# Unread products added to TensorE behind the last layer of a hybrid trunk

## The chip, the core and the metric

The kernel runs on one core of one Trainium2 chip. The metric is the device time of one execution in microseconds (us); the time before is 1177.72 us, the median of two runs (1177.52 and 1177.92). Five engines work side by side, each through its own instruction stream: TensorE (PE; its weight loads are listed apart as PEld), VectorE (DVE), ScalarE (ACT), GpSimd (POOL) and SyncE (SP, which issues DMAs here).

## What is computed

Two layers of a decoder trunk over 256 tokens of width 1024, in float32:

```python
proj = x @ w_in[l]                                  # 1024 -> 12800
y_a = short_conv_mixer(parts[3], parts[4], parts[5], conv_w[l])
y_b = dilated_attention_mixer(parts[6:6 + n_attn], positions)   # 3 groups of 8 heads of 64
y_c = chunked_spatial_gating(parts[6 + n_attn], parts[7 + n_attn], ...)
m = g_a * (y_a @ p_a[l]) + g_b * (y_b @ p_b[l]) + g_c * (y_c @ p_c[l])
x = layer_norm(ALPHA * x + m @ w_o[l], ln1_g[l], ln1_b[l])
h = jax.nn.silu(x @ w_gate[l]) * (x @ w_up[l])      # 1024 -> 2816
x = layer_norm(ALPHA * x + h @ w_down[l], ln2_g[l], ln2_b[l])
```

## The kernel before

Each float32 matrix product is made of three products of 12-bit parts in the type float32r: with h + l the two parts of an operand, h h' + h l' + l h'. Weights come from HBM in panels of up to 1 MB into one of three `raw` buffers (SP issues them, line 158) and are split there in pieces of 512 columns: ScalarE writes the high part `wh` (line 179), VectorE the low part `wl` (line 180). The pieces live in `slots`, 72 of 2 KB a partition, which the activations share.

Two patterns carry nearly all products. `feat` (lines 246 to 248, through `mm3`) has features on partitions: the weights are stationary (128x128), the activations move, 256 columns, one for each token; a panel of 256 features takes 2 x 8 x 3 = 48 products. `toks` (lines 266 to 268) has tokens on partitions: 128 tokens of an activation are stationary, the weights move, 512 columns (256 in the first two feed-forward blocks). Names in the profile stand as out<-moving,stationary or the reverse; `xh` and `xl` are the parts of x, `yah`, `ych`, `hh`, `mh` and their like those of branch results, hidden features and the merged branches, all kept in slots.

Where operands lie follows from the pools: `xh` and `xl` begin 160 bytes past a multiple of 512 in each partition, every slot and every `raw` buffer 224 bytes past one, and rows inside are multiples of 512 bytes apart. With "distance" for the moving operand's address less the stationary one's, modulo 512 bytes, `feat` on x has distance 448, `toks` on x has 64, and both have 0 where the activation lives in slots.

Between runs of products other work is placed by a clock of the program's own: transposes (lines 296, 612, 804; two to four in a row into a `trp` bank), attention's products (scores of 64 rows, lines 591 to 595; values of 64 weight columns, line 622). PSUM holds four `acc` banks and four `trp` banks, taken in turn.

The end: `down_last` finishes the last product into the four `acc` banks, a token tile after the other. For each half row VectorE adds it to x (`resid`, line 337) and takes statistics; `norm` (lines 313 to 327) follows for the tile, and SP stores each half (line 855). After that the program ends with a barrier of all engines.

Of the kernel before, what the change touches and what calls it, by code (L numbers as in the profile page):

```python
# [18 lines left out]
S = 256  # L19
# [20 lines left out]
# Weights: columns split at a time, panels loaded ahead.  # L40
PIECE = 512
RAW = 3
# Slots of 2 KB a partition; those that weights leave to others.
NS = 72
SPARE = 8
# TensorE time between two turns of the other engines' work, ns.
TICK = 1300
# Pieces of weights to have ready for splits to wait behind a layer norm.
# [5 lines left out]
# Steps of attention a turn.  # L54
PACE = 0.5

# Column layout of the constants.
# [8 lines left out]
# Pieces, of few bits each, of 2*pi and of (2**20, 2**9)/(2*pi) less its whole turns.  # L66
# [6 lines left out]
def constants():  # L73
    """Identity, masks and rotary frequencies: they depend on shapes alone."""
# [3 lines left out]
    # Attention keeps tokens ordered by their residue mod 2, in two tiles: a tile of queries sees  # L78
    # all keys of the first group, and of the dilated ones only the keys of its own tile.
# [16 lines left out]
def trunk(ctx: ExitStack, tc: tile.TileContext, a, out):  # L96
# [43 lines left out]
    # ---------------------------------------------------------------- weights  # L140
# [3 lines left out]
    class Panel:  # L144
        """Weights [kc * 128, nw], kept as 12-bit parts h + l in pieces of 512 columns."""
# [23 lines left out]
        def at(self, k, c, n):  # L169
            """Columns c..c+n of row block k, both parts."""  # L170
# [6 lines left out]
    def split(h, l, src):  # L177
        """h + l = src, both of them of 12 bits."""
        nc.scalar.activation(h, src, AF.Copy)  # L179
        V.tensor_tensor(l, src, h.bitcast(F32), op=OP.subtract)  # L180
# [15 lines left out]
    def used(n=1):  # L196
        """Pieces of weights done with."""
        free(2 * n)
# [6 lines left out]
    def soon(n, f):  # L205
        """f at the n-th turn from here."""
        timed.append((clock[1] + n, f))

    def tick():
        """Work of other engines, and attention, between runs of matmuls."""  # L210
# [33 lines left out]
    def mm3(o, hl, rhs_h, rhs_l, first, last):  # L244
        """o (+)= h.T @ (h' + l') + l.T @ h'."""
# [4 lines left out]
    def feat(p, rhs):  # L250
        """Features on partitions: (panel).T @ activations, a bank for two blocks."""
# [11 lines left out]
    def toks(ps, lhs, p, k, c, n, first, last):  # L263
        """Tokens on partitions: activations.T @ panel, one row block into one bank."""
# [10 lines left out]
    def by_residue(x):  # L275
        """Tokens (innermost) in the order of attention."""
# [15 lines left out]
    def to_features(t, q):  # L292
        """Half of x of a token tile, transposed and split."""
# [6 lines left out]
    # ---------------------------------------------------------------- layer norm  # L300
# [642 lines left out]
```

## Time and profile before

| | before |
|---|---|
| time, median of 2 runs | 1177.72 us |
| span of the profiled execution | 1174.9 us |
| PE busy | 1164.0 us, 99% of the span, 8884 products |
| PEld busy | 1101.0 us, 94% |
| DVE busy | 789.3 us, 67% |
| ACT busy | 622.8 us, 53% |
| POOL busy | 14.2 us, 1% |
| granted TensorE clock, mean | 0.999 of full speed |
| DMA | 222.41 MB, mean 189 GB/s |

The span runs from the first to the last instruction of one execution. A product's duration in the profile includes its way through the array, so durations overlap; what a run of products costs is read from starts, as the pitch from one start to the next. In a timeline row the columns are: start in us from the span's start, duration in us, engine, line, operation, out<-in, partitions x columns, count of instructions that the row merges, and in brackets the idle time before.

### The profile page before, as it was taken

How to read it: one execution, taken by the hardware profiler on the slowest of the kernel's cores; microseconds unless marked ns; L12 is line 12 of the kernel's file. 1: busy time of each engine (PE TensorE's matmuls, PEld its weight loads, DVE VectorE, ACT ScalarE, POOL GpSimd, SP SyncE). 2: the span in 40 equal slices, each digit the busy share in tenths (PEclk: the TensorE clock that was granted, in tenths of full speed). 3: DMA queues.
4: the chain of work that ended last, by engine and by line, in shares of the span. 5: the costliest groups of instructions: out<-in, count | busy, mean ns of one | idle time of the engine just before them, and what ended most of it. 6: DMA issues, size and time to landing. Idle time of an engine off the chain costs nothing.

```text
span 1174.9 us, 21651 instructions
## 1 busy us (share of the span) xinstructions
PE 1164.0 (99%) x8884; PEld 1101.0 (94%) x8884; DVE 789.3 (67%) x1426; ACT 622.8 (53%) x1126; POOL 14.2 (1%) x29
## 2 busy tenths in 40 slices
PE   9999999999999999999999999999999999999997
PEld 7899999999999899998888999999999999999985
DVE  6978886666755777556496677766676567764534
ACT  6666554676544466445185454546755444654530
POOL 0000000000000000000100000000000000000000
PEclk9999999999999999999999999999999999999999
DMA  9588554435857378448367664453566583774530
GB/s 343 202 258 251 171 167 146 142 126 197 265 178 235 111 228 281 171 146 317 113 215 250 181 188 135 151 172 109 177 216 204 194 251 108 253 234 160 176 111 36
DMA packets 180695, 222.41 MB, mean 189 GB/s; under 512 B 5456, under 2 KB 154228, under 8 KB 180596
## 3 DMA queue, kind: packets, MB, share of 16 engines
q1 hardware_dynamic: 178500, 214.66, 55.7%
q0 software_dynamic: 1952, 6.31, 1.9%
q8 instruction: 69, 1.13, 0.4%
q14 instruction: 30, 0.25, 0.1%
q10 hardware_dynamic: 144, 0.07, 0.0%
HBM read 213.67 MB, written 1.05 MB: 183 GB/s over the span
## 4 chain that ended last, share of the span: by engine, by line
PE 98%; DVE 1%; DMA 0%; ACT 0%; SPq 0%; issue 0%
PE acc L246 22%; PE acc L247 21%; PE acc L248 21%; PE acc L267 9%; PE acc L268 9%; PE acc L266 9%; PE acc L622 1%; PE trp L595 1%; PE trp L612 1%; PE trp L592 1%; PE acc L701 1%; PE trp L296 0%; DMA raw<-in_w_in 0%; PE trp L591 0%; PE trp L804 0%; PE trp L442 0%
## 5 line engine op out<-in xcount | busy, mean ns | idle before, releaser
L180 DVE TENSOR_TENSOR wl<-raw,wh 128x512 fp32r<-128x512 f32 x776 | 490.9, 686 | 179.8 <-ACT wh L179 171.2
L246 PE MATMUL acc<-xh,wh 128*128 128x256 f32 x1856 | 523.1, 282 | 0.0
L247 PE MATMUL acc<-xl,wh 128*128 128x256 f32 x1856 | 514.9, 277 | 0.0
L248 PE MATMUL acc<-xh,wl 128*128 128x256 f32 x1856 | 514.8, 277 | 0.0
L179 ACT ACTIVATE wh<-raw 128x512 fp32r<-128x512 f32 x776 | 432.1, 622 | 69.7 <-DMA raw<-in_w_in 26.5
L246 PEld LDWEIGHTS acc<-xh,wh 128*128 128x128 f32 x1856 | 348.8, 188 | 6.0 <-issue 2.1
L248 PEld LDWEIGHTS acc<-xh,wl 128*128 128x128 f32 x1856 | 349.8, 188 | 0.0
L247 PEld LDWEIGHTS acc<-xl,wh 128*128 128x128 f32 x1856 | 348.8, 188 | 0.1
L266 PE MATMUL acc<-wh,xh 128*128 128x512 f32 (+1 forms) x288 | 100.4, 349 | 0.3 <-ACT xh L179 0.3
L267 PE MATMUL acc<-wl,xh 128*128 128x512 f32 (+1 forms) x288 | 98.8, 343 | 0.2 <-DVE wl L180 0.2
L268 PE MATMUL acc<-wh,xl 128*128 128x512 f32 (+1 forms) x288 | 98.8, 343 | 0.0
L266 PE MATMUL acc<-wh,hh 128*128 128x512 f32 x176 | 68.6, 390 | 0.0
L268 PE MATMUL acc<-wh,hl 128*128 128x512 f32 x176 | 68.5, 389 | 0.0
L267 PE MATMUL acc<-wl,hh 128*128 128x512 f32 x176 | 68.5, 389 | 0.0
L266 PEld LDWEIGHTS acc<-wh,xh 128*128 128x128 f32 x288 | 54.7, 190 | 7.2 <-ACT wh L179 0.5
L267 PEld LDWEIGHTS acc<-wl,xh 128*128 128x128 f32 x288 | 54.8, 190 | 6.8 <-DVE wl L180 0.5
L268 PEld LDWEIGHTS acc<-wh,xl 128*128 128x128 f32 x288 | 54.7, 190 | 6.6 <-DVE xl L180 0.4
L599 ACT ACTIVATE p<-p,ml 128x512 f32<-128x512 f32 x32 | 23.3, 728 | 61.3 <-DVE ml L598 56.3
L179 ACT ACTIVATE hh<-hs 128x512 fp32r<-128x512 f32 x18 | 11.4, 634 | 64.3 <-DVE hs L823 64.3
L316 ACT ACTIVATE sd<-mv,eps 128x1 f32<-128x1 f32 x12 | 3.6, 298 | 72.4 <-DVE mv L313 72.4
L337 DVE SCALAR_TENSOR_TENSOR xt<-xt,acc 128x512 f32<-128x512 f32 x16 | 11.0, 685 | 44.5 <-PE acc L268 44.5
L268 PEld LDWEIGHTS acc<-wh,hl 128*128 128x128 f32 x176 | 33.0, 188 | 6.8
(148 smaller groups left out, 1329.1 us busy)
## 6 DMA issues: line engine op xcount, KB each, us to landing
raw<-in_w_in SPq DMA_DIRECT2D x99, 1024.0 KB, 5.3
raw<-in_w_gate SPq DMA_DIRECT2D x22, 1024.0 KB, 5.8
raw<-in_w_up SPq DMA_DIRECT2D x22, 1024.0 KB, 5.2
raw<-in_w_down SPq DMA_DIRECT2D x22, 1024.0 KB, 4.8
raw<-in_p_a SPq DMA_DIRECT2D x8, 1024.0 KB, 5.3
raw<-in_p_c SPq DMA_DIRECT2D x8, 1024.0 KB, 5.1
raw<-in_w_o SPq DMA_DIRECT2D x8, 1024.0 KB, 5.7
sw<-qk SPq DMA_DIRECT2D x96, 64.0 KB, 3.0
```

What stands on the lines that cost most here:

```text
L179: nc.scalar.activation(h, src, AF.Copy)
L180: V.tensor_tensor(l, src, h.bitcast(F32), op=OP.subtract)
L246: nc.tensor.matmul(o, lhsT=hl[0], rhs=rhs_h, start=first, stop=False)
L247: nc.tensor.matmul(o, lhsT=hl[0], rhs=rhs_l, start=False, stop=False)
L248: nc.tensor.matmul(o, lhsT=hl[1], rhs=rhs_h, start=False, stop=last)
L266: nc.tensor.matmul(ps, lhsT=lhs[0], rhs=h, start=first, stop=False)
L267: nc.tensor.matmul(ps, lhsT=lhs[0], rhs=l, start=False, stop=False)
L268: nc.tensor.matmul(ps, lhsT=lhs[1], rhs=h, start=False, stop=last)
L592: nc.tensor.matmul(ps[:, c], lhsT=q[d, b, own], rhs=qk[hf, "kh"][d, b, keys], start=False, stop=True)
L595: nc.tensor.matmul(ps[:, c], lhsT=q[d, b, own], rhs=k[d, b, keys], start=True, stop=True)
L599: nc.scalar.activation(p, p, AF.Exp, bias=ml[:, 0:1], scale=-1.0, accum_out=ml[:, 1:2])
L612: nc.tensor.transpose(ps[:, i * 128:(i + 1) * 128], p[:, i * 128:(i + 1) * 128], ident)
```

## The change

Behind the last layer's program, two `raw` buffers `W` are filled with ones by POOL, and products follow on TensorE whose results nothing reads. A first loop runs over 18 distances `d` from 0 to 480 bytes: `mm3` as in `feat`, on the parts of x as moving operand and a piece of `W` as stationary one, whose offset `o` is set so that the distance is `d`; 24 products, two transposes (`kick(2)`), and the 24 again. A second loop does the pattern of `toks` at the same distances, 12 products each, with x stationary and `W` moving. Then come products of 64 rows, of 64 columns and of both, as attention has them, on x's parts and on the constants (float32), and four transposes. The other hunks take comments and docstrings out; line numbers stay as they were up to line 920.

```diff
@@ -920,6 +920,60 @@
     assert not hooks and not slow and live[0] == 0, (len(hooks), live)
 
 
+
+    W = []
+    for i in range(2):
+        w = wp.tile([128, 2048], F32R, tag="raw", name="w")
+        nc.gpsimd.memset(w.bitcast(F32), 1.0)
+        W.append(w)
+
+    def kick(n):
+        ps = trp()
+        for i in range(n):
+            nc.tensor.transpose(ps[:, i * 128:(i + 1) * 128], con[:, C_M:C_M + 128], ident)
+
+    dist = (0, 16, 32, 48, 64, 96, 128, 160, 192, 224, 256, 288, 320, 352, 384, 416, 448, 480)
+    ps = acc()
+    for d in dist:
+        o = (-64 - d) % 512 // 4
+        for again in range(2):
+            for k in range(8):
+                wk = [w[:, k * 256 + o:k * 256 + o + 128] for w in W]
+                mm3(ps[:, :S], wk, *xf(k), k == 0, k == 7)
+            if again == 0:
+                kick(2)
+    for d in dist:
+        o = (-64 + d) % 512 // 4
+        for k in range(4):
+            h, l = (w[:, k * 256 + o:k * 256 + o + 512] for w in W)
+            lhs = xtok(k, 0)
+            nc.tensor.matmul(ps, lhsT=lhs[0], rhs=h, start=k == 0, stop=False)
+            nc.tensor.matmul(ps, lhsT=lhs[0], rhs=l, start=False, stop=False)
+            nc.tensor.matmul(ps, lhsT=lhs[1], rhs=h, start=False, stop=k == 3)
+    b4 = [trp() for i in range(4)]
+    up, dn = slice(0, 64), slice(64, 128)
+    m = con[:, C_M:]
+    for i in range(6):
+        nc.tensor.matmul(b4[0][:, :256], lhsT=xh[up, 0, :128], rhs=xh[up, 1, :], start=True, stop=True)
+    for i in range(3):
+        for j, r in enumerate((up, dn)):
+            nc.tensor.matmul(b4[j][:, :256], lhsT=xh[r, 0, :128], rhs=xh[r, 1, :], start=True, stop=True)
+    for i in range(4):
+        for j, r in enumerate((up, dn)):
+            nc.tensor.matmul(b4[j + 2][:, i % 4 * 128:(i % 4 + 1) * 128], lhsT=m[r, :128], rhs=m[r, 256:384], start=True, stop=True)
+    for i in range(4):
+        for j, r in enumerate((up, dn)):
+            for q in (up, dn):
+                nc.tensor.matmul(b4[j][q, i * 64:(i + 1) * 64], lhsT=m[r, q], rhs=m[r, 256:320], start=True, stop=True)
+    for i in range(4):
+        for q in (up, dn):
+            nc.tensor.matmul(b4[2][q, i * 128:(i + 1) * 128], lhsT=m[:, q], rhs=m[:, 256:384], start=True, stop=True)
+    for i in range(4):
+        for q in (up, dn):
+            nc.tensor.matmul(b4[3][q, i * 64:(i + 1) * 64], lhsT=m[:, q], rhs=m[:, 256:320], start=True, stop=True)
+    kick(4)
+
+
```

In the order of TensorE's instructions the new ones stand behind the last product of `down_last` (a row is line, operation, out<-moving operand, partitions x columns; the weights aren't named; line 246 to 248 is `mm3`, `w` one of the two buffers `W`):

```order
 L267 MATMUL acc<-wl,hh_13579 128x512
 L268 MATMUL acc<-wh,hl_13580 128x512
-L939 UNCONDITIONAL_BRANCH
+L246 MATMUL acc<-xh,w 128x256
+L247 MATMUL acc<-xl,w 128x256
+L248 MATMUL acc<-xh,w 128x256
```

The program went to its closing branch there; now the first of 1172 products follow. Their end, on the same engine:

```order
+L952 MATMUL acc<-w,xl 128x512
+L957 MATMUL trp<-xh 128x256 x6
+L960 MATMUL trp<-xh 128x256 x6
+L963 MATMUL trp<-con 128x128 x8
+L967 MATMUL trp<-con 64x64 x16
+L970 MATMUL trp<-con 64x128 x8
+L973 MATMUL trp<-con 64x64 x8
+L933 MATMUL trp<-con 128x128 x4
+L993 UNCONDITIONAL_BRANCH
```

The last forms stand behind the second loop, and only then does TensorE reach its closing branch. On POOL, whose last work was the load of the last norm's parameters:

```order
 L306 DMA gb<-in_ln_g 128x512 x2
 L306 DMA gb<-in_ln_b 128x512 x2
-L939 UNCONDITIONAL_BRANCH
-L939 ISA
+L927 MEMSET w 128x2048 x2
+L993 UNCONDITIONAL_BRANCH
+L993 ISA
```

The two fills come behind those loads. The first product waits for VectorE (the residual that reads the first `acc` bank) and for POOL's first fill, the third product for the second fill. The streams of ScalarE, VectorE and SP are as before.

## Rows read from the trace of the kernel before

**Rows 1.** The page: granted clock in 40 slices (tenths), and chain by engine.
```profile
PEclk9999999999999999999999999999999999999999
PE 98%; DVE 1%; DMA 0%; ACT 0%; SPq 0%; issue 0%
```
**Rows 2.** Timeline, the end: last product, first residual behind it, last norm step, store.
```profile
1165.77 0.39 PE L268 MATMUL acc<-wh,hl 128*128 128x512 f32 x1
...
1166.19 0.69 DVE L337 SCALAR_TENSOR_TENSOR xt<-xt,acc 128x512 f32<-128x512 f32 x1 [4.02 <-PE acc L268]
...
1170.89 0.75 DVE L327 SCALAR_TENSOR_TENSOR xt<-xt,sd,gb 128x512 f32<-128x512 f32 x1
1171.67 0.33 SPq L855 DMA_DIRECT2D out<-xt  x1
```
**Rows 3.** DMA issues: count, KB each, median us to landing.
```profile
out<-xt SPq DMA_DIRECT2D x4, 256.0 KB, 2.0
```
**Rows 4.** Timeline: last splits, POOL's last load, residual that frees the first bank.
```profile
1126.52 2.73 DVE L180 TENSOR_TENSOR wl<-raw,wh 128x512 fp32r<-128x512 f32 x4 [2.11 <-ACT wh L179]
...
1132.32 0.54 POOL L306 DMA_DIRECT2D gb<-in_ln_b  x1 [0.23 <-issue]
...
1149.88 0.69 DVE L337 SCALAR_TENSOR_TENSOR xt<-xt,acc 128x512 f32<-128x512 f32 x1 [20.63 <-PE acc L268]
```
**Rows 5.** Groups by line and form, VectorE's fills: busy us, mean ns of one.
```profile
L898 DVE MEMSET idle<- 128x64 f32 x1 | 0.1, 112 | 0.8 <-PEq L931 0.8
L899 DVE MEMSET eps<- 128x1 f32 x1 | 0.1, 59 | 0.0
```
**Rows 6.** Timeline, layer 1's gates and branches: where runs on x and slots begin.
```profile
865.22 0.29 PE L246 MATMUL acc<-xh,wh 128*128 128x256 f32 x1
...
881.56 0.28 PE L246 MATMUL acc<-yah,wh 128*128 128x256 f32 x1
...
895.94 0.29 PE L246 MATMUL acc<-xh,wh 128*128 128x256 f32 x1
...
895.94 0.19 PEld L247 LDWEIGHTS acc<-xl,wh 128*128 128x128 f32 x1
```
**Rows 7.** Timeline, layer 1's feed-forward: first product behind a transpose's successor, and the end.
```profile
1008.40 0.28 PE L247 MATMUL acc<-xl,wh 128*128 128x256 f32 x1
...
1106.15 0.39 PE L266 MATMUL acc<-wh,hh 128*128 128x512 f32 x1
```
**Rows 8.** Timeline, two transposes amid products of 256 columns.
```profile
420.94 0.38 PE L804 MATMUL trp<-con,hs 128*128 128x128 f32 x2
421.07 0.36 PE L266 MATMUL acc<-wh,xh 128*128 128x256 f32 x1
421.28 0.28 PE L267 MATMUL acc<-wl,xh 128*128 128x256 f32 x1
```
**Rows 9.** Timeline, token products of 512 columns: starts of runs on x and hidden features.
```profile
585.79 0.39 PE L266 MATMUL acc<-wh,xh 128*128 128x512 f32 x1
...
594.72 0.49 PE L296 MATMUL trp<-con,xt 128*128 128x128 f32 x3
...
1160.56 0.39 PE L266 MATMUL acc<-wh,hh 128*128 128x512 f32 x1
```
**Rows 10.** Timeline, attention's products of 64 rows, and of 64 weight columns.
```profile
119.68 0.28 PE L591 MATMUL trp<-stack 128*128 128x256 f32 x1
119.89 0.38 PE L592 MATMUL trp<-kh,stack 64*128 64x256 f32 x1
120.11 0.60 PE L595 MATMUL trp<-qk,qk 64*128 64x128 f32 x4
120.65 0.38 PE L246 MATMUL acc<-xh,wh 128*128 128x256 f32 x1
...
164.02 1.09 PE L622 MATMUL acc<-pT,va 128*64 128x128 f32 x16
165.04 0.39 PE L246 MATMUL acc<-xh,wh 128*128 128x256 f32 x1
```

## Prediction

> **What bounds the kernel now.** I read the page first, then the end of the timeline, then stretches of TensorE's timeline. The page's chain of work that ended last is TensorE for 98% of the span, and its clock row stands at full speed (2.4 GHz) in every slice of 40 [rows 1]. So the time is the sum of TensorE's pitches (start of one product to the start of the next), and a product added at the end is paid in full unless it fits under something that already follows TensorE's last product. Such a thing exists and is short: the last product starts at 1165.77 us; VectorE's residual and layer norm follow until 1171.64, and the store is issued at 1171.67 for 0.33 us [rows 2] and lands some 2.0 us later [rows 3], at 1174.0; the span closes at 1174.87, another 0.9 us. From 1166.00 (1165.77 plus one pitch of 0.23) to 1174.87 are 8.9 us of cover; what TensorE does beyond that lengthens the run. The profiled execution's span is 1174.87 us; the median of the two runs is 1177.72, so 2.85 us lie around the span, which I keep.
>
> **What the change adds.** Nothing is moved or removed; by the order, the engines' programs are the same up to the end. Added are two fills on POOL and 1172 products on TensorE, with no reader. They start without a wait, if three things are in time. The accumulator bank that the first run takes is free once the residual of the first half row has read it, by 1150.57 us [rows 4]. The two raw buffers are free after the last splits, which end at 1129.25 [rows 4]. The fills stand on POOL behind its last load, which ends there at 1132.86 [rows 4]. No fill of this size is in the trace; the nearest rows are VectorE's fills of 64 columns (112 ns) and of one (59 ns) [rows 5], 0.84 ns a column, so 1.7 us for 2048 columns. Taken four times as slow, two fills still end near 1147, 19 us ahead of 1166.0. They cost nothing as long as each takes under 16.5 us; TensorE waits for whatever the two take beyond 33 us.
>
> **The price of a product of the layers' pattern.** The same instruction, 128x128 weights against 256 columns, runs at three steady pitches in the trace. With x as the moving operand (its address lies 448 bytes ahead of the weights', modulo 512): 144 products from 865.22 to 881.56, 113.5 ns each. With the split branch results as the moving operand (distance 0, since they and the weights live in the same slots): 120 products from 881.56 to 895.94, 119.8 ns each [rows 6]. And with x again, same distance 448, but in layer 1's feed-forward: 830 products from 1008.40 to 1106.15, 117.8 ns each [rows 7]. The engine, the clock and the shapes are the same in all three. What differs is the distance, or, at one distance, what came just ahead: this last stretch began behind two transposes. The weight load of the next product starts together with the product that runs (both at 895.94 [rows 6]), so the two read SBUF at the same time, and I read the 4 to 6 ns as the price of their meeting. The change samples 18 distances, each with 24 products, two transposes, and 24 more, so that both states are met.
>
> The Trainium skill's page "TensorE: Matmul & The Clock Gate" (Step-by-step: what each phase is for) says that TensorE has two independent SBUF read ports, and that loading the next weights does not take bandwidth from the running matmul. By that rule neither distance nor history would matter, every product would run at the lowest pitch, and the time would be rival 2's. The trace does not agree: 113.5 against 117.8 and 119.8 ns [rows 6, 7].
>
> For distances that the trace lacks I take the middle of the lowest and the highest steady pitch, 116.6 ns, and keep both ends. First loop: 18 x 2 x 8 x 3 = 864 products x 116.6 ns = **100.7 us** (98.1 to 103.5).
>
> **The kicks.** Two transposes between such products: they start at 420.94, and the second product behind them starts at 421.28 [rows 8]. That is 0.34 us for two transposes and one product; less the product's own 0.12, a kick costs 0.22 us (the product behind them starts early, but its successor is late by some 0.09: a weight load that isn't hidden). Eighteen of them: **4.0 us**. From the fifth on they wait for the kick of four kicks before, which lies 200 products (23 us) back, so that wait is over when they come.
>
> **The token pattern.** 18 x 4 x 3 = 216 products of 512 columns. Weights from the slots' own distance 0: 24 products from 1160.56 to the last one's start at 1165.77 [rows 2, 9], 23 pitches of 226.5 ns. x as the stationary operand at distance 64: 39 products from 585.79 to 594.72, 229.0 ns [rows 9]. Here twice the columns leave the load more room, and the two distances differ by 1% only. I take 228 ns: **49.2 us** (48.9 to 49.5).
>
> **The forms of attention.** Products of 64 rows, of 64 columns, or both; those on float32 operands are two entries each in the trace, as the 16 entries of line 622 for eight products show.
> - 12 products of 64 rows by 256 columns: line 592's takes 0.22 us to the next start, but a float32 one follows it; among themselves I take the ordinary 0.12, 1.4 us (0.7 if upper and lower halves run side by side; 2.6 at 0.22).
> - 8 products of 64 rows by 128 columns, 16 entries: four such take 0.54 us from 120.11 to 120.65 with the change of shape behind them [rows 10], 0.11 without it: 1.8 us (0.9 to 2.2).
> - 16 products of 64x64, 32 entries: bounded by line 622's 0.064 us an entry (16 from 164.02 to 165.04 [rows 10]): 2.0 us if nothing runs side by side, half of it if it does; 1.4.
> - 8 products of 64 weight columns by 128, 16 entries like line 622's: 1.0 us. The same with 64 columns: 0.5 to 1.0, 0.7.
> - 4 transposes, 0.4, and about five changes of shape at 0.1 each (line 591's 0.21 against 0.11 [rows 10]), 0.5.
>
> Sum **7.3 us**; 4.4 with everything side by side. If every one of the 80 float32 entries took 0.135 (0.54 over four) and the 12 took 0.22, it would be 14.
>
> **The sum.** 100.7 + 4.0 + 49.2 + 7.3 = 161.2 us. TensorE ends at 1166.00 + 161.2 + 0.2 (the last transpose's own end) = 1327.4; the store has landed 153 us earlier. With the 0.9 us of closing the span is 1328.3, with the 2.85 around it **1331.2 us**. With all low ends 155.4 us and 1325; with all high ends 171.3 us and 1341.
>
> **Rivals.**
> 1. *A distance uncovers the weight load.* Behind a kick one product's pitch is 0.21 us (421.07 to 421.28 [rows 8]), that is, the load is not hidden at all. If a distance kept it so, its 48 products would cost 48 x (0.207 - 0.117) = 4.3 us more; four such distances give 1348, all eighteen 1409. Against it: three distances and both states are in the trace, and the worst steady pitch is 119.8. Chance 0.10.
> 2. *Distance doesn't matter*: 864 x 113.5 ns and 216 x 226.5 ns, 3.0 us less, 1328. For it: 113.5 is the commonest pitch. Against it: rows 6 and 7. This is the rule of the Trainium skill's page above; by the trace so far it has little. Chance 0.08.
> 3. *POOL's fills come late.* At 30 us each TensorE would stand 27 us, 1358, and its clock could fall besides. Against it: rows 4 and 5. Chance 0.02.
> 4. *Not slower*: the added work hides beside the last norm and store. That decides at 8.9 us of TensorE time for no change at all, and at 8.9 + 23.6 = 32.5 us for 2%, which is about what a measurement of this kernel can tell from no change. The built program holds 1080 plain products, so each would have to take under 0.03 us, a quarter of any pitch of this shape in the trace; the same price would hold if they were dropped as unread, but they stand in TensorE's program. Chance 0.01.
>
> **How the numbers follow.** The forecast has 0.79, with its own range 1325 to 1341. The other cases lie on both sides of it: rival 2 inside, rival 1 above. I end the range at 1322 below (distances better than any seen, by 4 ns on each of 864 products) and at 1346 above (three to four uncovered distances); what is left out is most of rival 1, rival 3 and the misjudged ends, some 0.15. Slower by over 2% holds 0.985, within 2% 0.01, faster 0.005: there is nothing in the change that could shorten the first 1166 us.
>
> **What would show it.** TensorE goes on from 1166.0 without a gap, at full clock; in the first loop, pitches between 113 and 120 ns that change with the distance, and for some distances between the 24 products ahead of the kick and the 24 behind it; kicks of 0.22 us; the second loop flat near 228 ns; the last form section near 7 us; the chain ends on TensorE. I am wrong if a distance shows a steady pitch beyond 125 or below 112 ns, if the 512-column pitch moves by over 3% with the distance, or if TensorE waits for POOL at the start.

## The result, and the profile after

The changed kernel takes 1330.87 us, the median of two runs (1329.92 and 1331.82), against 1177.72: a ratio of 1.1302, 95% interval 1.1282 to 1.1323. The forecast was 1331.2. The profiled execution is the one of 1329.92 us; its span is 1328.1 us (forecast 1328.3).

The page of the changed kernel, TensorE's busy row, the granted clock in 40 slices and the chain of work that ended last, which answer to [rows 1]:

```profile
PE 1325.3 (100%) x10096; PEld 1252.2 (94%) x10096; DVE 789.6 (59%) x1426; ACT 621.6 (47%) x1126; POOL 17.7 (1%) x31
...
PEclk9999999999999999999999999999999999999999
...
PE 99%; DMA 0%; ACT 0%; issue 0%; SPq 0%; DVE 0%
```

The busy times of VectorE and ScalarE are those of before; only TensorE and POOL have grown, and the chain is TensorE to the end. The layers have not moved. From TensorE's timeline in layer 1's feed-forward, which answers to [rows 7] (start, duration, operation, out<-in):

```profile
1008.35 0.28 PE L247 MATMUL acc<-xl,wh 128*128 128x256 f32 x1
...
1106.10 0.39 PE L266 MATMUL acc<-wh,hh 128*128 128x512 f32 x1
```

Both stand 0.05 us earlier than before, 830 products at 117.8 ns between them. At the place where the added work begins, TensorE's timeline and POOL's [rows 2, 4]:

```profile
1165.71 0.39 PE L268 MATMUL acc<-wh,hl 128*128 128x512 f32 x1
1165.94 0.28 PE L246 MATMUL acc<-xh,w 128*128 128x256 f32 x1
```

```profile
1132.96 3.56 POOL L927 MEMSET w<- 128x2048 f32 x2 [0.16 <-issue]
```

The first added product follows the last old one by 0.23 us, without an idle time in brackets: nothing is waited for. The two fills take 1.78 us each [rows 5 for the nearest of before] and end at 1136.5, 29 us early. Three stretches of TensorE's timeline in the first loop follow: the kick at distance 0 [rows 8], the run ahead of the kick at distance 32, and both runs at distance 192.

```profile
1168.81 0.38 PE L933 MATMUL trp<-con 128*128 128x128 f32 x2
1168.95 0.36 PE L246 MATMUL acc<-xh,w 128*128 128x256 f32 x1
1169.15 0.28 PE L247 MATMUL acc<-xl,w 128*128 128x256 f32 x1
...
1177.81 0.28 PE L246 MATMUL acc<-xh,w 128*128 128x256 f32 x1
...
1180.61 0.38 PE L933 MATMUL trp<-con 128*128 128x128 f32 x2
...
1213.15 0.28 PE L246 MATMUL acc<-xh,w 128*128 128x256 f32 x1
...
1215.98 0.38 PE L933 MATMUL trp<-con 128*128 128x128 f32 x2
...
1216.32 0.28 PE L247 MATMUL acc<-xl,w 128*128 128x256 f32 x1
...
1218.94 0.28 PE L246 MATMUL acc<-xh,w 128*128 128x256 f32 x1
```

A kick and the product behind it take 0.34 us, so a kick costs 0.22. The 24 products at distance 0 take 1165.94 to 1168.81, 119.7 ns each; at 32 they take 2.80 us, 116.7 each; at 192 they take 2.83 us, 117.9 each, ahead of the kick, and behind it 23 of them take 2.62 us, 113.9 with the settling at the start. The settled pitch of each run (its first intervals left out), worked out from starts in the same timeline as the mean of the last 15 intervals within each run of 24, in ns:

| distance | ahead of the kick | behind it |
|---|---|---|
| 0, 256 | 120.0 | 119.9 |
| 16 | 119.8 | 117.3 |
| 32, 288 | 116.7 | 116.9 |
| 48 | 116.7 | 116.8 |
| 64, 320 | 117.8 | 117.8 |
| 96, 352 | 120.2 | 119.7 |
| 128, 160, 384, 416 | 118.7 | 118.7 |
| 192, 448 | 117.8 | 113.3 |
| 224, 480 | 118.5 | 118.1 |

Distances that differ by 256 give the same. At 192 and 448 the two transposes changed the pitch by 4.5 ns, at 16 by 2.5, elsewhere by 0.5 at most. The loop takes 1165.94 to 1272.00, 106.06 us. The second loop, TensorE's timeline at distances 0, 96 and 256 and at its last product [rows 9]:

```profile
1272.00 0.40 PE L950 MATMUL acc<-w,xh 128*128 128x512 f32 x1
...
1285.89 0.40 PE L950 MATMUL acc<-w,xh 128*128 128x512 f32 x1
...
1288.47 0.39 PE L952 MATMUL acc<-w,xl 128*128 128x512 f32 x1
...
1299.89 0.40 PE L950 MATMUL acc<-w,xh 128*128 128x512 f32 x1
...
1302.39 0.39 PE L952 MATMUL acc<-w,xl 128*128 128x512 f32 x1
```

Eleven pitches from the first to the last product of a distance are 2.58 us at 96 (234.5 ns) and 2.50 at 256 (227.2). The loop ends at 1322.26, after 50.26 us, 232.7 ns a product. The forms of attention, TensorE's timeline with rows of one line merged (the count is behind the x; float32 operands are two entries each) [rows 10]:

```profile
1322.26 0.73 PE L957 MATMUL trp<-xh 64*128 64x256 f32 x4
...
1323.41 1.07 PE L963 MATMUL trp<-con 64*128 64x128 f32 x15
1324.41 0.69 PE L967 MATMUL trp<-con 64*64 64x64 f32 x32
1325.04 1.09 PE L970 MATMUL trp<-con 128*64 128x128 f32 x16
1325.96 0.63 PE L973 MATMUL trp<-con 128*64 128x64 f32 x16
1326.53 0.66 PE L933 MATMUL trp<-con 128*128 128x128 f32 x4
```

From 1322.26 to the last transpose's end at 1327.18 are 4.92 us. By the single starts, the entries of line 963 come in pairs 1 ns apart from the sixth on, a pair every 0.11 us; those of line 967 in fours within 20 ns; those of lines 970 and 973 in pairs 7 ns apart. So they run side by side. The span closes 1.0 us later, at 1328.1.

### The profile page after: what moved, and what is told of

It is laid out like the page before. It is cut to its first block, busy times and chain, and to the rows that moved or that the text cites. A ratio compares the mean times of both kernels' runs of the same rounds, so it can differ in the third digit from the quotient of the medians.

```text
span 1328.1 us, 24085 instructions
## 1 busy us (share of the span) xinstructions
PE 1325.3 (100%) x10096; PEld 1252.2 (94%) x10096; DVE 789.6 (59%) x1426; ACT 621.6 (47%) x1126; POOL 17.7 (1%) x31
## 3 DMA queue, kind: packets, MB, share of 16 engines
q1 hardware_dynamic: 178500, 214.66, 49.2%
## 4 chain that ended last, share of the span: by engine, by line
PE 99%; DMA 0%; ACT 0%; issue 0%; SPq 0%; DVE 0%
PE acc L246 22%; PE acc L248 21%; PE acc L247 21%; PE acc L268 8%; PE acc L267 8%; PE acc L266 8%; PE acc L950 1%; PE acc L952 1%; PE acc L951 1%; PE acc L622 1%; PE trp L595 1%; PE trp L612 1%; PE trp L592 1%; PE acc L701 1%; PE trp L296 0%; PE trp L933 0%
## 5 line engine op out<-in xcount | busy, mean ns | idle before, releaser
L246 PE MATMUL acc<-xh,w 128*128 128x256 f32 x288 | 82.2, 286 | 0.0
L248 PE MATMUL acc<-xh,w 128*128 128x256 f32 x288 | 80.8, 281 | 0.0
L247 PE MATMUL acc<-xl,w 128*128 128x256 f32 x288 | 80.8, 281 | 0.0
L247 PEld LDWEIGHTS acc<-xl,w 128*128 128x128 f32 x288 | 54.4, 189 | 0.0
L246 PEld LDWEIGHTS acc<-xh,w 128*128 128x128 f32 x288 | 54.3, 188 | 0.0
```

What stands on the lines that cost most here:

```text
L246: nc.tensor.matmul(o, lhsT=hl[0], rhs=rhs_h, start=first, stop=False)
L247: nc.tensor.matmul(o, lhsT=hl[0], rhs=rhs_l, start=False, stop=False)
L248: nc.tensor.matmul(o, lhsT=hl[1], rhs=rhs_h, start=False, stop=last)
```

## The experiments

Two theories were open behind the total. Theory A: a product's pitch is set by the distance between the two operands, plus a state that a pause in the stream can change. Theory B: the operands' own addresses, or distance alone, set it. Besides, the plain sum, the cover of the fills and the share of columns in the price wanted a test of their own. The kernels with repeated fills, shifted operands, the history of transposes, fine distances, several widths and eight insertions were timed once each; what they show is read from their traces.

### The plain sum: without the first loop

```diff
     for d in dist:
-        o = (-64 - d) % 512 // 4
-        for again in range(2):
-            ...
-    for d in dist:
         o = (-64 + d) % 512 // 4
```

> The changed kernel without its first loop (864 products and 18 times two transposes); the layers are computed in full. In the changed kernel's trace that loop takes 106.1 us. If the added time is a plain sum on TensorE, the time is 1330.9 - 106.1 = 1224.8 us, 1.040 of before. If part of the loop's time were hidden, or the rest ran otherwise without it, it would lie higher or lower by that part.

Measured: 1224.53 us, ratio 1.040 (1.0383 to 1.0418). TensorE's timeline at the join:

```profile
1167.29 0.39 PE L268 MATMUL acc<-wh,hl 128*128 128x512 f32 x1
1167.52 0.39 PE L942 MATMUL acc<-w,xh 128*128 128x512 f32 x1
```

The second loop follows the layers directly, and the medians differ by 1330.87 - 1224.53 = 106.3 us, the loop's own 106.06 to within what medians of two chips differ. In this profiled execution the layers run 1.6 us later from their first products on, as far as one execution differs from another here (below, under the terms of the sum). The loop's time is paid in full, and nothing else is slowed by it.

### The fills' cover: twelve fills for each buffer

```diff
-        nc.gpsimd.memset(w.bitcast(F32), 1.0)
+        for again in range(12):
+            nc.gpsimd.memset(w.bitcast(F32), 1.0)
```

> The changed kernel, with each of POOL's two fills done twelve times; the layers are computed in full. One fill takes 1.78 us in the changed kernel, so they end at 1132.96 + 24 x 1.78 = 1175.7 us, past the cover, which ends at 1165.9. By the prediction's reckoning TensorE's third added product waits some 9.6 us, and the time is 1340.5. If the granted clock falls in the wait, the first products behind it run at half speed and the time is a few us more, by the trace's own rows after the pause. If the fills were no condition of the start, the time stays 1330.9.

Measured: 1343.57 us. POOL's row, the first product that waits (its idle time and releaser in brackets), and a stretch of the windows table (from:to, length, busy us and counts of PE, PEld, DVE, ACT, POOL, then granted clock, DMA share, GB/s):

```profile
1132.87 44.65 POOL L928 MEMSET w<- 128x2048 f32 x24 [0.16 <-issue]
...
1177.57 0.58 PE L248 MATMUL acc<-xh,w 128*128 128x256 f32 x1 [11.34 <-POOL w L928]
```

```profile
1178.00:1180.00 2.00, 2.00 (x11) 2.00 (x11) 0.00 (x0) 0.00 (x0) 0.00 (x0) 0.50 0.04 8
```

The fills end at 1177.5, and TensorE stands 11.3 us in front of its third product. Behind that pause the granted clock is at half, 1.2 GHz, and 20 products start 213 ns apart (1177.95 to 1182.22), 0.094 us more each than the 120 ns of this distance at full clock: another 1.9 us. The time is 3.1 us over the 1340.5 of the plain sum, and the trace has two reasons for it: these 1.9 us, and a wait of 11.3 instead of 9.6, because a repeated fill takes 1.86 us and not 1.78 (44.65 for 24). So the cover of 33 us was real, and the third rival's price is shown with its second part, the clock.

### Distance or address: both operands shifted together

```diff
-    for d in dist:
-        o = (-64 - d) % 512 // 4
+    for d in (0, 32, 96, 192):
+        for a0 in (0, 32, 64, 128):
+            m, o = 128 + a0 // 4, 128 + (a0 - d) // 4
...
+                    mv = [w[:, k * 256 + m:k * 256 + m + 256] for w in W]
+                    mm3(ps[:, :S], wk, mv[1], mv[0], k == 0, k == 5)
```

> The layers are computed in full; in place of the added products stand 576 others, on the buffers of ones alone: distances 0, 32, 96 and 192, each with both operands shifted together by 0, 32, 64 and 128 bytes, 18 products, two transposes, 18 products. If the distance between the operands sets the pitch, each distance keeps its pitch under all four shifts: about 120.0 ns at 0, 116.7 at 32, 119.7 to 120.3 at 96, 117.8 or 113.3 at 192, to within 1 ns in the last ten of a run. If the stationary operand's own address sets it, a shift by 64 bytes has to move distance 0 from the pitch of one class to that of another (of 120.0, 118.7, 117.8), and the four shifts of one distance differ by 2 to 5 ns. Some 67 us of products, time near 1246 us either way.

Measured: 1240.22 us. The settled pitch (here of the last ten intervals) at distance 0 is 120.0 ns under all four shifts, ahead of the kick and behind it (eight runs); at 32 it is 116.2 to 117.1 and at 96 it is 119.8 to 120.1, eight runs each. So at these three distances the addresses themselves don't matter, only their distance. At 192 it is 113.3 in five runs and 117.8 to 117.9 in the other three. Of the four runs there that follow two transposes, two are at 117.8 (shifts 0 and 32) and two at 113.3 (64 and 128). TensorE's timeline at shifts 32 and 64, each from the second product behind the transposes to the first of the next shift:

```profile
1226.54 0.28 PE L247 MATMUL acc<-w 128*128 128x256 f32 x1
...
1228.54 0.28 PE L246 MATMUL acc<-w 128*128 128x256 f32 x1
...
1230.94 0.28 PE L247 MATMUL acc<-w 128*128 128x256 f32 x1
...
1232.89 0.28 PE L246 MATMUL acc<-w 128*128 128x256 f32 x1
```

2.00 us and 1.95 us for 17 pitches at the same distance, 117.8 and 114.5 ns with the settling at the start. This distance has two states, each of which holds to the end of its run. Between one shift and the next there are no transposes, and yet the state turned there three times: from 117.8 to 113.3 at shifts 32 and 64, and back at 128.

### What chooses the state: runs behind 1 to 4 transposes

```diff
+    for d in (448, 64, 32):
+        o = (-64 - d) % 512 // 4
+        run(112, 1)
+        run(o, 4)
+        for n in (1, 2, 3, 4, 2, 2, 2, 1, 4):
+            kick(n)
+            run(o)
```

`run(o, n)` is the first loop's 24 products n times (twice without n); `run(112, 1)` is 24 at distance 0. It stands in place of both loops and the forms.

> The layers are computed in full; in place of the added products stand runs at one distance (448, then 64, then 32), 96 or 48 products each, parted by 1, 2, 3, 4, 2, 2, 2, 1 and 4 transposes. If the state is chosen where a run begins, each run at 448 settles within some five products at 113.3 or at 117.8 ns and holds that to its end, the choice differing from transposes to transposes; distance 64 shows 113.3 after some of them too, as it did in layer 0's first feed-forward blocks; 32 stays at 116.7 to 116.9. If the pitch drifts with time or follows other engines' work, runs change in their middle, or every run at one distance shows the same pitch, since all other engines rest here.

Measured: 1369.98 us. At 448, settled pitches: 117.8 behind the run at distance 0 (96 products); 113.3 behind two transposes, four times of four; 117.8 behind one (twice) and three; behind four 113.3 once and 117.8 once. At 64: 113.3 behind the run at distance 0 and behind four transposes (twice), 117.8 behind one, two and three. At 32: 116.4 to 116.9 always. TensorE's timeline at the two runs of 96, 448 first, each from its first product to the transpose behind it:

```profile
1170.08 0.28 PE L246 MATMUL acc<-xh,w 128*128 128x256 f32 x1
...
1181.39 0.27 PE L933 MATMUL trp<-con 128*128 128x128 f32 x1
...
1236.57 0.28 PE L246 MATMUL acc<-xh,w 128*128 128x256 f32 x1
...
1247.45 0.27 PE L933 MATMUL trp<-con 128*128 128x128 f32 x1
```

11.31 and 10.88 us for 96 products, 117.8 and 113.3 ns. A state lasts as long as the stream runs on, and the number of transposes is not by itself what chooses it (four gave both at 448, as two did at 192 in the run with shifted operands).

### Fine distances

```diff
-    for d in dist:
+    for d in (4, 8, 12, 16, 24, 40, 56, 176, 184, 188, 192, 196, 200, 208, 240, 248, 252):
```

The second loop and the forms are left out.

> The layers are computed in full; in place of the added products stands the first loop at 17 other distances, 4 to 56, 176 to 208 and 240 to 252 bytes, in steps down to 4. If a meeting of two reads that step through rows of memory decides, neighbours within 8 bytes of 0 keep 120 ns and neighbours of 192 keep the 113.3 ns state behind the kick. If only distances that are whole multiples of 64 bytes have the two states, 188 and 196 show 116 to 119 ns both ahead of and behind the kick. All pitches stay between 113 and 121 on either theory; a steady pitch beyond 125 would be the uncovered load that the prediction set as a rival.

Measured: 1270.70 us. The pitches that follow are means of the last eleven intervals. The two states of 192 (117.7 and 113.3) are not shared by its neighbours: 188 gives 118.5, 196 gives 120.0 and 118.5, 184 gives 118.0. The highest settled pitch is 123.2 ns, at 24 ahead of the kick (117.9 behind it); the lowest besides 113.3 is 115.5 at 248. None is beyond 125. Neither theory of the expectation held as a whole: of the neighbours of 0, 4 keeps 120, but 8 and 252 are at 117.5 to 118.5; and a pitch that differs ahead of the kick and behind it is not left to multiples of 64, since 16 (120.2 and 117.3), 24 and 56 (118.0 and 116.6) have it too.

### Fewer columns, and more

```diff
+    for d in (0, 64, 96, 192):
+        for n in (512, 384, 256, 192, 128, 64):
+            for k in range(12):
+                s = 128 + k % 4 * 256
+                o = s - d // 4
+                wk = [w[:, o:o + 128] for w in W]
+                nc.tensor.matmul(ps[:, :n], lhsT=wk[0], rhs=W[1][:, s:s + n], start=k == 0, stop=False)
+                nc.tensor.matmul(ps[:, :n], lhsT=wk[1], rhs=W[0][:, s:s + n], start=False, stop=k == 11)
```

It stands in place of both loops and the forms.

> The layers are computed in full; in place of the added products stand runs of 24 on the buffers of ones, at distances 0, 64, 96 and 192, with 512, 384, 256, 192, 128 and 64 columns. If what is lost is lost to the weight load, the excess over 0.4427 ns a column (113.3 at 256) is one amount for each load, 0 to 8 ns, no larger at 512 columns than at 256; and with few columns the pitch stops falling at the load's own time, which lies below 113 ns. If it is lost to each stretch of moving columns, the excess doubles from 256 to 512 columns (13 ns at distance 0, 226.7 + 13 = 240) and halves at 128.

Measured: 1254.14 us. Settled pitches (last eleven intervals) in ns:

| distance | 512 columns | 384 | 256 | 192 | 128 | 64 |
|---|---|---|---|---|---|---|
| 0 | 226.7 | 173.4 | 120.0 | 111.6 | 111.5 | 111.6 |
| 64 | 228.6 | 173.4 | 117.8 | 111.9 | 111.4 | 111.6 |
| 96 | 233.0 | 176.9 | 120.4 | 111.6 | 111.5 | 111.6 |
| 192 | 233.6 | 174.5 | 113.3 | 111.5 | 111.6 | 111.6 |

From 192 columns down the pitch no longer falls. I read the 111.6 ns as the pace of the weight load; no run took the load away to show it. At 512 columns the distances differ by 6.9 ns, no less than at 256, and the order is another: 192 is the cheapest at 256 columns and the dearest at 512, 0 the cheapest at 512 and one of the two dearest at 256. At 384 they differ by 3.5. So the price of distance does not grow with the columns, and 512 of them don't hide it, but it is not one fixed amount for each product either.

One thing was not expected by either theory. TensorE's timeline behind the narrow products at distance 0, and the windows table there (columns as above):

```profile
1188.60 0.63 PE L942 MATMUL acc<-w 128*128 128x512 f32 x1
1189.03 0.63 PE L943 MATMUL acc<-w 128*128 128x512 f32 x1
```

```profile
1185.00:1187.50 2.50, 2.50 (x25) 2.50 (x24) 0.00 (x0) 0.00 (x0) 0.00 (x0) 1.00 0.02 7
1187.50:1190.00 2.50, 2.50 (x11) 2.00 (x11) 0.00 (x0) 0.00 (x0) 0.00 (x0) 0.60 0.00 0
```

The granted clock fell to half, and seven products of 512 columns in a row (1188.17 to 1191.16) started 427 ns apart instead of 227 to 229, though TensorE had issued without a gap: ahead of the fall stood 72 products of 192, 128 and 64 columns, 1179.83 to 1187.79. The same 72 stood again ahead of the runs of 512 columns at 96 and at 192 (1201.95 to 1209.90, 1222.70 to 1230.66), and there the clock stayed at full. So what made it fall the first time is open.

### Using the state: transposes ahead of a long run

In layer 1's feed-forward 768 products on x run at 117.8 ns from the fourth hidden block on. At 113.3 they would take 3.4 us less. The kernel before, with two (or, in a second run, one) unread transposes ahead of that block's gate panel:

```diff
+                if final and j == 3:
+                    kp = trp()
+                    for i in range(2):
+                        nc.tensor.transpose(kp[:, i * 128:(i + 1) * 128], con[:, C_M:C_M + 128], ident)
```

> The kernel before, without the added products, and with two unread transposes ahead of the gate panel of block 3 in layer 1's feed-forward. In the kernel before, the 768 products from there run at 117.8 ns. If the state of distance 448 is chosen behind an interruption, they settle at 113.3 as they did behind two transposes in six of six cases so far (distances 192 and 448 in the changed kernel, 448 four times in the history experiment): 768 x 4.5 ns less 0.22 us for the transposes, 3.2 us or 0.27% faster than before. If the slower pitch of that stretch comes from splits and transfers beside it, it stays, and the time grows by 0.2 us.

> The same with one transpose. Behind one transpose distance 448 settled at 117.8 in both cases of the history experiment. If the choice follows the interruption alone, the stretch stays at 117.8 and the time at that of before plus 0.1 us. If other work disturbs the choice, it may fall to 113.3 all the same (3.3 us faster).

Measured: 1178.39 and 1177.71 us against 1177.20, ratios 1.0004 (0.9995 to 1.0013) and 1.0003 (0.9994 to 1.0012); those of the medians, 1.0010 and 1.0004, lie in the same intervals. The state did not change. TensorE's timeline with two transposes, the second product behind them and the first behind the stretch:

```profile
1017.61 0.28 PE L247 MATMUL acc<-xl,wh 128*128 128x256 f32 x1
...
1107.94 0.39 PE L266 MATMUL acc<-wh,hh 128*128 128x512 f32 x1
```

767 products in 90.33 us, 117.8 ns. What two transposes had done at this distance in all four cases of the history run they did not do here; so the theory that their number chooses the state fell. The "six of six" of the expectation had left out the run with shifted operands, where two transposes at 192 were followed by 117.8 in two cases of four. The kernel before speaks against it as well. Layer 0's feed-forward, the same stretch of the program, also begins behind two transposes (at 429.86), and from the second product behind them it runs at the other pitch, 836 products at 113.4 ns where layer 1's [rows 7] take 117.8:

```profile
430.20 0.28 PE L247 MATMUL acc<-xl,wh 128*128 128x256 f32 x1
...
524.97 0.39 PE L266 MATMUL acc<-wh,hh 128*128 128x512 f32 x1
```

### The branches at another distance

Slots 2304 bytes apart instead of 2048 (66 of them instead of 72), with the split branch results 192 bytes into theirs, so that the branch products run at distance 192 instead of 0:

```diff
-NS = 72
+NS = 66
...
-        return sl.tile([128, 512], dt, tag="slot", name=name)
+        wide = sl.tile([128, 576], dt, tag="slot", name=name)
+        o = 48 if name[:2] in ("ya", "yb", "yc") else 0
+        return wide[:, o:o + 512]
```

> The kernel before, without the added products; slots are 2304 bytes apart and 66 instead of 72, and the split branch results lie 192 bytes into theirs, so that the 960 products of the three branches have distance 192 instead of 0. If the distance sets the pitch there too, these products fall from 119.8 to 113.3 or 117.8 ns, 1.9 to 6.2 us in all, and nothing else changes as long as six slots fewer don't delay splits (TensorE's idle time stays as it is). If what they pay comes from their lying in slots (other engines write there), they stay at 119.8 and the time at that of before.

Measured: 1180.93 us, ratio 1.0035 (1.0023 to 1.0048): slower by its interval, though far under 2%. TensorE's timeline, a run of branches, the gates behind it (144 products on x), and the next branches [rows 6]:

```profile
883.96 0.28 PE L248 MATMUL acc<-yah,wh 128*128 128x256 f32 x1
...
898.09 0.28 PE L248 MATMUL acc<-xh,wh 128*128 128x256 f32 x1
...
915.05 0.28 PE L248 MATMUL acc<-yah,wh 128*128 128x256 f32 x1
```

The 120 branch products went from 119.8 to 117.8 ns (14.38 to 14.13 us), as the distance says. But the gates, whose distance had not changed, went from 113.5 to 117.8 (16.34 to 16.96 us), six times in the two layers. Distances 192 and 448 are the same modulo 256, so branches and gates had become one unbroken run in one state, the dearer one; in the kernel before, each gate run follows a run at distance 0 and is at 113.3. By the trace the layers take 1.7 us more from the first products to the last; the interval of the ratio says 2.7 to 5.7, and where the rest lies is not shown.

### A run at distance 0 as the switch

That result points at a run at distance 0 as what turns the state. Layer 1's feed-forward of the kernel before, with unread products at distance 0 (hidden features on hidden features) or transposes ahead of eight of its blocks:

```diff
+                what, n = {3: ("zero", 6), 4: ("kick", 2), 5: ("zero", 3), 6: ("kick", 4), 7: ("zero", 12), ...
...
+                    if what == "kick":
+                        nc.tensor.transpose(kp[:, i * 128:(i + 1) * 128], con[:, C_M:C_M + 128], ident)
+                    else:
+                        nc.tensor.matmul(kp[:, :S], lhsT=hT[0][i % 2][:, 0, :128], rhs=hT[1][0][:, 0, :], ...
```

> The kernel before, without the added products, and with an unread interruption ahead of each gate panel of blocks 3 to 10 in layer 1's feed-forward: 6 products at distance 0 on the hidden features' slots (block 3), 2 transposes (4), 3 products at distance 0 (5), 4 transposes (6), 12 at distance 0 (7), 2 transposes (8), 6 at distance 0 (9), 3 transposes (10); 96 products at distance 448 stand between. If the run ahead sets the state, as a run at distance 0 ahead of layer 1's gates does (113.5 in six of six), those behind 6 and 12 products at distance 0 settle at 113.3 and those behind transposes at either pitch, each holding for its 96 products. If only the exact instant at which the two reads start counts, the outcomes follow no such order. If the stretch is slow for another cause (slots, splits, transfers), all eight stay at 117.8. Time within 3 us of before in every case.

Measured: 1179.22 us, beside 1179.76 of the kernel before on the same chip. TensorE's timeline behind the first six products (line 821 is theirs) and at the next transposes:

```profile
1017.57 0.28 PE L821 MATMUL trp<-hh,hh 128*128 128x256 f32 x1
1017.69 0.28 PE L821 MATMUL trp<-hh,hl 128*128 128x256 f32 x1
1017.81 0.29 PE L246 MATMUL acc<-xh,wh 128*128 128x256 f32 x1
...
1028.72 0.38 PE L819 MATMUL trp<-con 128*128 128x128 f32 x2
```

Ahead of the six the pitch is 117.8, behind them 96 products take 10.91 us, 113.6 with the settling (113.3 settled), and it stays at 113.3 through all the seven insertions that follow, transposes too. So the six turned the state. The same with the six, or three, alone:

```diff
-                what, n = {3: ("zero", 6), 4: ("kick", 2), ...
+                what, n = {3: ("zero", 3)}.get(j, ("", 0)) if final else ("", 0)
```

> The kernel before with 6 unread products at distance 0 ahead of block 3's gate panel in layer 1's feed-forward, and nothing else. Theory (a run at distance 0 turns the state, and the state then holds): the 768 products behind them, at a distance of 448 modulo 512, go from 117.8 to 113.3 ns, 768 x 4.45 = 3.4 us; the 6 products cost 0.7; so 2.7 us less than before, a ratio near 0.9977. Rival (the turn seen after the last layer does not repeat here): the pitch stays at 117.8 and the kernel is 0.7 us longer, a ratio near 1.0006.

> As the run with 6, with 3 products at distance 0 in that place. If three are enough to turn the state: 3.4 us less 0.35, so 3.0 us less than before, a ratio near 0.9974. If it takes six: the pitch stays at 117.8 and the kernel is 0.4 us longer, 1.0003. Three were so far seen only behind a run that was already at 113.3, so they do not tell yet.

Measured: 1174.24 us with six and 1174.28 with three, against 1177.44; both ratios 0.9974 (0.9963 to 0.9984, and 0.9966 to 0.9983). TensorE's timeline with three:

```profile
1015.83 0.28 PE L821 MATMUL trp<-hh,hh 128*128 128x256 f32 x1
...
1016.18 0.29 PE L246 MATMUL acc<-xh,wh 128*128 128x256 f32 x1
...
1103.24 0.39 PE L266 MATMUL acc<-wh,hh 128*128 128x512 f32 x1
```

768 products in 87.06 us, 113.4 ns (settled 113.3), where the kernel before takes 117.8; with six it is 87.06 as well. Three unread products of 0.35 us in all save 3.4 us in the stretch, 3.1 in the whole: a version 0.26% faster than before, real by its interval though far under 2%. In the same place one and two transposes had left the pitch at 117.8, so it takes more than a break in the stream. Three products at another distance were not tried there, so it is not shown that distance 0 is what did it. The layers' other runs at 117.8 were not tried either.

## Why the prediction was right, step by step

**The mechanism.** TensorE is the clock of this kernel, nothing hides the added products, and the time rose by their pitches, less the 8.9 us of cover at the end. This is shown by the chain [rows 1 and its answer] and by the kernel without the first loop, 106.3 us shorter for a loop of 106.06.

**The terms of the sum.** The end came out at 1327.18 instead of 1327.4, but by errors that cancel, so that the total came so close is luck:

| term | predicted | measured | difference |
|---|---|---|---|
| start behind the layers | 1166.00 | 1165.94 | -0.06 |
| first loop, kicks included | 104.7 | 106.06 | +1.4 |
| second loop | 49.2 | 50.26 | +1.1 |
| forms and the last end | 7.5 | 4.92 | -2.6 |
| closing | 0.9 | 1.0 | +0.1 |
| median less profiled span | 2.85 | 2.77 | -0.1 |

The last term needs a word. In every execution whose span is listed, 1.7 to 1.9 us lie around the span; the rest of the 2.85 is that executions differ by 1 to 2 us in the first microseconds, where TensorE's first transposes run at half or at full clock and wait for x a little longer or shorter, and keep the difference to the end. The two of the changed kernel have spans of 1328.1 and 1330.0. So half a microsecond of a difference between two medians is not to be read closely.

**First loop: mis-sized.** The kicks cost 0.22 as predicted. The product cost 118.2 ns, not 116.6. The step that failed is the middle between the lowest and the highest pitch seen, which gives both the same weight: of the 36 runs two have the 113.3, and the others lie between 116.7 and 120.2. The 117.8 of the long stretch [rows 7] would have given 105.8, but nothing in the trace of before singled it out, since layer 0's stretch, as long, ran at 113.4. That layer also shows that "this last stretch began behind two transposes" does not tell the two pitches apart: both began so. The two readings under it held all the same: distance matters, and at one distance the pitch can change behind two transposes (117.8 to 113.3 at 192 and 448).

**Second loop: the step failed.** "Here twice the columns leave the load more room" made it flat near 228; it goes from 227.2 at 256 to 234.2 at 96 (means of 12), 3%, which is where the prediction had put its own refutation of this point. The run with six widths shows that the room did not help: the excess over the cheapest distance goes up to 6.9 ns at 512 columns, 3.5 at 384 and 7.1 at 256, so it does not shrink steadily as the columns grow. Why the order of the distances changes with the columns is open. The two rows that I had [rows 9] were the two cheapest distances, 0 and 64.

**Forms: mis-sized.** Side by side they cost 4.65 us up to the last start, near the low end of 4.4 (the items of the prediction add up to 7.2, not 7.3). Products of 64 rows in upper and lower halves, and of 64 columns, share the array: the 16 of 64x64 (32 entries) take 1324.41 to 1325.04, 0.63 us, where I had taken 1.4 between "nothing" and "half"; the eight of line 963 take 1.2 us where I had 1.8, the twelve of 64 rows by 256 columns 0.94 where I had 1.4. These times hold the changes of shape, for which I had 0.5 more. The bound was right and the choice inside it was not.

**Fills.** 1.78 us each against 1.7 from VectorE's rows; covered, and the cover's end was measured with twelve of them.

**The rivals.** No distance uncovers the load (1): the highest steady pitch is 120.2 here and 123.2 among the fine ones. That distance doesn't matter (2) is refuted by eight runs at each of three distances: 120.0 at 0 under all shifts against 116.7 at 32. The Trainium skill's page "TensorE: Matmul & The Clock Gate" (Step-by-step: what each phase is for) says that loading the next weights does not take SBUF read bandwidth from the running matmul. By that rule alone the two pitches would be the same, and they are 3.3 ns apart; whether the two reads are where the difference arises is not shown. Fills that come late (3) cost what the rival said plus the clock. That the work hides (4) had nothing for it.

**What was only argued.** I read the 4 to 6 ns as the meeting of the weight load with the running product in SBUF. The runs fit it: at 0, 32 and 96 only the distance counts and not the addresses, the price has a period of 256 bytes, and the 111.6 ns that I read as the load's own pace lie just under these pitches. No run took the load away, so the place of the meeting is not shown. And what chooses between the two states stays open. A run at distance 0 gave 113.3 behind it in the six gate runs of the kernel before, in the run of eight insertions, and with six and with three alone; but at the head of the history run 24 such products were followed by 117.8 at 448. Two transposes turned it from 117.8 to 113.3 behind the layers and in layer 0 of the kernel before, and from 113.3 to 117.8 in layer 1 (33 products that settled at 113.3 ahead of the two at 1008.06) and twice among the shifted operands. The transposes put into layer 1's feed-forward, one to four of them, left it alone in six places of six. And a shift of both operands, with neither transposes nor another distance between, turned it three times.

## What to carry to other kernels

Where TensorE's stream has no gap, added products cost their pitch. Where the trace has several steady pitches for one shape, none of them is sure for a case not seen (the two longest stretches here had 113.4 and 117.8): count how often each occurs, keep both ends as the range, sum by term and keep the terms, since a right total can rest on errors that cancel. Where the same instruction has two pitches in one trace, look at the distance between its operands modulo 256 bytes and at what ran ahead of the stretch: 4% of a stretch of 90 us could be had for three unread products. Products of half the rows or half the columns, their halves in turn, ran side by side here and are to be counted so.

## What was not expected of the hardware

- The pitch of a float32r product of 256 columns depends on the operands' distance with a period of 256 bytes: 113.3 to 120.2 ns at multiples of 16, up to 123.2 at 24. At 64 and 192 there are two steady states, 113.3 and 117.8, that last until the stream changes (transposes, another distance, other addresses); transposes turn the state only sometimes. At 16, 24 and 56 there were two pitches as well; at 0, 32, 96 and 128 one was seen.
- Of the four distances compared, the best at 256 columns (192: 113.3) is the worst at 512 (233.6); distance 0 is the best at 512 (226.7) and near the worst at 256 (120.0).
- With 128x128 weights loaded anew each time, a float32r product of 192, 128 or 64 columns took 111.6 ns; fewer columns made it no cheaper.
- The granted clock fell to half, 427 ns for 512 columns, behind 8 us of narrow products that were issued without a gap; behind the same products it stayed at full two times more.
